# Two products from one moving operand: merge gates, branch and output projections, delta gates

## The chip, the cores and the metric

The kernel runs on one core of a Trainium2 chip. The metric is device time in microseconds (us) of one launch. Engines in the text: PE is TensorE (matmuls; PEld its weight loads), DVE is VectorE, ACT is ScalarE, POOL is GpSimd, SP issues the DMAs. Matmuls write PSUM, in banks of 512 f32 columns on 128 partitions; ACT and DVE read the banks and write SBUF.

## The reference

All data are f32, 256 tokens of width 1024. First a block of a hybrid mixer (two attention kinds, whose outputs of width 512 are raised to the model width, gated and summed) and product-key experts; then, with 16 meta tokens ahead, a banded attention layer and a gated delta-rule layer. The lines whose computation the change touches:

```
# hybrid mixer: y_fox, y_nsa are the outputs of the two attentions
g = sigmoid(merge_logit).reshape(B_, S_, 2, 1024)         # merge_logit: columns of h @ w_in
ys = stack([y_fox, y_nsa], axis=2)
up = einsum('bsnc,ncd->bsnd', ys, w_branch)
merged = sum(g * up, axis=2)
return merged @ w_out                                      # the caller adds the residual
# delta layer
u = rms_norm(h, norm_w) @ w_in                             # q, k, v, z, b, a
... gated delta rule of q, k, v gives o ...
... the normalised o is multiplied by silu(z), then o @ w_out
```

## The kernel before

**Products.** To keep f32 accuracy on PE, every f32 operand is split into a part `hi` (rounded to fp32r) and the rest `lo`, and a product is three: hi·hi, lo·hi, hi·lo (`mm3`, L277). The stationary operand is a weight block of 128x128, the moving one the activations transposed, [128 of the width, token columns]. `proj_t` (L284) makes one output block of 128x256 in PSUM: for each k (a 128-slice of the width) three matmuls of 256 columns.

**Weights.** `unit` (L263) brings one unit of weights, 128x1024 f32 (512 KB): a DMA by SP into `raw` (4 buffers), ACT copies it to `hi` (L269), DVE subtracts to get `lo` (L270); hi and lo have 3 buffers each. One unit is the weights of one output block over 8 k, or, in the branch projection, of two output blocks over 4 k.

**The stages in question.** They follow each other late in the mixer and in the second half of the delta layer. Merge gates (L670 to L676): 16 units, two of which fill the two halves of a bank (`pj_ps`, 2 buffers); DVE multiplies the bank by R (the token's norm) into `mg`, ACT takes tanh. Branch (L678 to L691): 8 units, for q = 0..3 one of each branch; a unit fills a bank with its two output blocks; DVE computes (mg + 1) * bank (scalar_tensor_tensor, L687) into `up`, sums the two branches' `up` (L690), and `split` (ACT L274, DVE L275) gives `me`, hi and lo. Output projection (L692 to L696): 8 units on `me`, two per bank; DVE computes 0.5 * bank + xT. Delta gates (`gates`, L1605): 16 units, each through `proj` into a bank of `pj`, and ACT takes silu (L1330) straight from it; between them stand the matmuls and copies of the delta rule's substitution (`r`, `pr`, `zt`, `rn`).

**Order.** The program is written in Python in this order, and the framework fixes each engine's order of instructions at build time by its own estimates of times (`schedule_with_timeline_sim=True`, L1782). A buffer is reused after its last reader (`reuse_waits="tile"`, L200), by a semaphore; each engine takes its instructions in the fixed order.

Of the kernel before, what the change touches and what calls it, by code (L numbers as in the profile page):

```python
# [6 lines left out]
F32 = mybir.dt.float32  # L7
F32R = mybir.dt.float32r
# [3 lines left out]
AF = mybir.ActivationFunctionType  # L12
ALU = mybir.AluOpType
# [4 lines left out]
T = 256  # L18
M = 16
L = M + T  # L20
KD = D // 128
# [169 lines left out]
class Net:  # L191
# [81 lines left out]
    def split(self, hi, lo, src):  # L273
        self.nc.scalar.activation(hi, src, AF.Copy)  # L274
        self.nc.vector.tensor_sub(lo, src, hi)  # L275

    def mm3(self, out, a, b, start, stop, **kw):  # L277

        mm = self.nc.tensor.matmul
        mm(out, a[0], b[0], start=start, stop=False, **kw)  # L280
        mm(out, a[0], b[1], start=False, stop=False, **kw)  # L281
        mm(out, a[1], b[0], start=False, stop=stop, **kw)  # L282
# [92 lines left out]
    def mixer(self, WARM=12):  # L375
        nc, ap = self.nc, self.ap
# [3 lines left out]
        h1T = self.hp.tile([128, KD, T], F32, name="h1T")  # L380
        self.h1T = h1T
        yf = self.xh.tile([128, 2, 4, T], F32R, name="yf", tag="xh")
        yn = self.xl.tile([128, 2, 4, T], F32R, name="yn", tag="xl")
        A = self.pool("mixA", side="right")
        W = self.pool("mixW", side="right")
        pj = self.pool("pj", bufs=2, space=PSUM)
# [3 lines left out]

        xT = A.tile([128, KD, T], F32, name="xT")
        nc.sync.dma_start(xT[:, 0:2], ap["xT"][:, 0:2])
        hh = A.tile([128, KD, T], F32R, name="hh", tag="ah")
        hl = A.tile([128, KD, T], F32R, name="hl", tag="al")
        units = iter(range(ap["w_t1"].shape[0]))
        nxt = lambda: self.unit(ap["w_t1"][next(units)])
        w = nxt()
# [3 lines left out]
        ps = sc.tile([128, 512], F32, name="warm", tag="sc")  # L401
# [5 lines left out]
        hT = (hh, hl)  # L407
# [7 lines left out]
        for m in range(0, 4, 2):  # L415
            ps = pj.tile([128, 2, T], F32, name="pj_ps", tag="pj")
            for j in range(2):
                self.proj_t(ps[:, j], nxt(), hT)
            if m == 0:
                R = A.tile([128, T], F32, name="R")  # L420
                self.rstd(R, xT, T, W, sc, "sc", load=False)
                Rb = R[:, None, :].to_broadcast([128, 2, T])
# [9 lines left out]
                z = W.tile([8, T], F32, name="fz")  # L432
# [26 lines left out]
            for f in range(2):  # L459
                s = slice(64 * f, 64 * f + 64)  # L460
                nc.vector.tensor_mul(kz[s, 2 * m + f:2 * m + 4:2], ps[s], Rb[s])
        for m in range(0, 4, 2):
            ps = pj.tile([128, 2, T], F32, name="pj_ps", tag="pj")
# [37 lines left out]
        yf = yf[:, 0], yf[:, 1]  # L501
        for i in range(2):
            n = 128 * (i + 1)
            ti = slice(i * 128, n)
            nh = 512 // n
            y = yp.tile([128, 4, 128], F32, name="y_ps", tag="yf")
            for h0 in range(0, 8, nh):
                ps = sc.tile([128, nh, n], F32, name="sc_ps", tag="sc")
                for j in range(nh):
                    h = h0 + j  # L510
# [9 lines left out]
                for j in range(nh):  # L520
                    h = h0 + j
# [147 lines left out]

        mg = A.tile([128, 16, T], F32, name="mg", tag="mg")  # L670
        for b in range(0, 16, 2):
            ps = pj.tile([128, 2, T], F32, name="pj_ps", tag="pj")
            for j in range(2):
                self.proj_t(ps[:, j], nxt(), hT)
            nc.vector.tensor_mul(mg[:, b:b + 2], ps, Rb)
            nc.scalar.activation(mg[:, b:b + 2], mg[:, b:b + 2], AF.Tanh, scale=0.5)  # L676

        me = [A.tile([128, KD, T], F32R, name="me" + n, tag="a" + n) for n in ("h", "l")]  # L678
        for q in range(4):
            ups = []  # L680
            for br, yy in ((0, yf), (1, yn)):
                w = self.unit(ap["w_br"][2 * q + br])
                ps = pj.tile([128, 2, T], F32, name="pj_ps", tag="pj")
                for j in range(2):
                    self.proj_t(ps[:, j], w, yy, ks=range(4), off=j * 512)
                up = W.tile([128, 2, T], F32, name="up", bufs=3)
                nc.vector.scalar_tensor_tensor(up, mg[:, 8 * br + 2 * q:8 * br + 2 * q + 2], 1.0, ps,  # L687
                                               op0=ALU.add, op1=ALU.mult)
                ups.append(up)
            nc.vector.tensor_add(ups[0], ups[0], ups[1])  # L690
            self.split(me[0][:, 2 * q:2 * q + 2], me[1][:, 2 * q:2 * q + 2], ups[0])  # L691
        for b in range(0, KD, 2):  # L692
            ps = pj.tile([128, 2, T], F32, name="pj_ps", tag="pj")
            for j in range(2):
                self.proj_t(ps[:, j], self.unit(ap["w_o1"][b + j]), me)
            nc.vector.scalar_tensor_tensor(h1T[:, b:b + 2], ps, 0.5, xT[:, b:b + 2], op0=ALU.mult, op1=ALU.add)  # L696
        self.dump("h1T", h1T)
        self.x2 = (self.xh.tile([128, KD, T], F32R, name="x2h", tag="xh"),
                   self.xl.tile([128, KD, T], F32R, name="x2l", tag="xl"))
# [527 lines left out]
    def delta(self, NZ=2, AH=4, KN=8, SS=1, SR=3, SW=3):  # L1227
# [17 lines left out]

        nh, nl = [A.tile([128, KD, L], F32R, name=n) for n in ("nh3", "nl3")]
        gd = self.d("g_dn")

        def normalise(k):
# [4 lines left out]
        def proj(ts=slice(0, L)):  # L1256
            ps = pj.tile([128, 512], F32, name="pj_ps", tag="pj")
            n = ts.stop - ts.start
            u = next(units)
            a = (hh, hl) if u <= KN else (nh, nl)  # L1260
            self.proj_t(ps[:, :n], self.unit(ap["w_t3"][u]), (a[0][:, :, ts], a[1][:, :, ts]))
            return ps[:, :n]
# [64 lines left out]
        def silu(raw, after=None, src=None):  # L1327

            with self.tc.issue_after(self.last), self.tc.issue_after(after or self.last):
                return nc.scalar.activation(raw, raw if src is None else src, AF.Silu).ins  # L1330
# [273 lines left out]

        def gates(z):  # L1605
            for j in range(4):
                silu(z[:, j], src=proj(slice(M, L)))
                yield

        sz = []  # L1610
# [175 lines left out]
```

## Time and profile before

| | us |
|---|---|
| median of 3 runs | 1470.3 (1469.41 to 1471.21) |
| the profiled execution | 1475.74 |
| its span | 1473.7 |
| PE busy in the span | 1445.8 (98%) |
| DVE busy | 1067.3 (72%) |
| ACT busy | 797.2 (54%) |

The times of single instructions come from the profiled execution. PE's busy time is modelled at the ends of matmuls, which overlap; the distance between starts is the pace. "a<-b" is the tile written and the tiles read; "128x256" is partitions by columns; a bracket at the end of a timeline row is the idle time of the engine before the instruction and who ended it.

### The profile page before, as it was taken

To read this page: it belongs to the slowest core of one execution; us is meant where nothing else is said; L and a number is where in the kernel's file an instruction comes from. 1 tells how busy PE (TensorE), PEld (TensorE's weight loads), DVE (VectorE), ACT (ScalarE), POOL (GpSimd) and SP (SyncE) were. 2 spreads that over 40 slices of the span, in tenths; PEclk is the share of its full clock that TensorE was granted. 3 is DMA by queue.
4 is the path that set the end of the run, shared out by engine and by line. 5 is a ranking of instruction groups with operands and counts; after the bars stand their busy time and mean duration, and the time that the engine had idled before them with its cause. 6 is when DMAs were issued, how large, how long until landed. Compare 5 with 4: busy or idle time off the path is not lost.

```text
span 1473.7 us, 27105 instructions
## 1 busy us (share of the span) xinstructions
PE 1445.8 (98%) x10635; PEld 1325.1 (90%) x10635; DVE 1067.3 (72%) x2124; ACT 797.2 (54%) x1372; POOL 73.5 (5%) x106
## 2 busy tenths in 40 slices
PE   9999999999999999999999999999999989999998
PEld 8788999999999999999888888888898989899777
DVE  7666577789948888998555555555876798985466
ACT  5566445545544444444444445454686667764364
POOL 0000000000000000000000000000113024000020
PEclk9999999999999999999999999999999999999899
DMA  6442464555655555555666666666442445435013
GB/s 229 141 146 85 143 186 150 173 167 171 195 178 159 162 154 171 157 151 170 195 190 197 193 192 197 198 189 197 143 126 76 145 129 158 144 127 156 21 43 114
DMA packets 72223, 229.19 MB, mean 156 GB/s; under 512 B 16048, under 2 KB 16464, under 8 KB 72096
## 3 DMA queue, kind: packets, MB, share of 16 engines
q1 hardware_dynamic: 71408, 225.69, 50.1%
q8 instruction: 83, 1.36, 0.4%
q0 software_dynamic: 400, 1.46, 0.3%
q10 hardware_dynamic: 288, 0.33, 0.1%
q14 instruction: 44, 0.36, 0.1%
HBM read 225.31 MB, written 2.13 MB: 154 GB/s over the span
## 4 chain that ended last, share of the span: by engine, by line
PE 93%; ACT 3%; DVE 2%; issue 1%; DMA 1%; POOL 0%; SPq 0%; ACTq 0%; DVEq 0%
PE pu_ps L280 10%; PE pu_ps L281 9%; PE pu_ps L282 9%; PE acc L280 8%; PE acc L281 8%; PE acc L282 8%; PE pj_ps L280 8%; PE pj_ps L282 8%; PE pj_ps L281 8%; PE pt_ps L898 2%; PE out L280 1%; PE tr_ps L366 1%; PE out L281 1%; PE out L282 1%; ACT hi L269 1%
## 5 line engine op out<-in xcount | busy, mean ns | idle before, releaser
L269 ACT ACTIVATE hi<-raw 128x1024 fp32r<-128x1024 f32 x422 | 445.8, 1058 | 432.2 <-PE pu_ps L281 167.8
L270 DVE TENSOR_TENSOR lo<-raw,hi 128x1024 fp32r<-128x1024 f32 x422 | 518.6, 1230 | 198.8 <-ACT hi L269 197.3
L280 PE MATMUL pu_ps<-x2h,hi 128*128 128x256 f32 x1152 | 330.8, 288 | 0.1
L281 PE MATMUL pu_ps<-x2l,hi 128*128 128x256 f32 x1152 | 326.4, 284 | 0.2 <-DVE x2l L275 0.2
L282 PE MATMUL pu_ps<-x2h,lo 128*128 128x256 f32 x1152 | 325.9, 283 | 0.0
L281 PEld LDWEIGHTS pu_ps<-x2l,hi 128*128 128x128 f32 x1152 | 221.0, 192 | 0.4 <-DVE x2l L275 0.4
L280 PEld LDWEIGHTS pu_ps<-x2h,hi 128*128 128x128 f32 x1152 | 220.5, 192 | 0.3 <-ACT x2h L274 0.3
L282 PEld LDWEIGHTS pu_ps<-x2h,lo 128*128 128x128 f32 x1152 | 220.7, 192 | 0.0
L281 PE MATMUL acc<-lo,ch 128*128 128x512 f32 x512 | 198.8, 389 | 0.0
L282 PE MATMUL acc<-hi,cl 128*128 128x512 f32 x512 | 198.2, 389 | 0.0
L280 PE MATMUL acc<-hi,ch 128*128 128x512 f32 x512 | 139.0, 389 | 0.0
L280 PE MATMUL pj_ps<-hh,hi 128*128 128x256 f32 (+1 forms) x432 | 125.7, 295 | 5.0 <-DVE cpad L1310 2.6
L282 PE MATMUL pj_ps<-hh,lo 128*128 128x256 f32 (+1 forms) x432 | 126.0, 293 | 0.5 <-DVE lo L270 0.5
L281 PE MATMUL pj_ps<-hl,hi 128*128 128x256 f32 (+1 forms) x432 | 125.9, 293 | 0.7 <-DVE hl L326 0.6
L282 PEld LDWEIGHTS acc<-hi,cl 128*128 128x128 f32 x512 | 96.1, 188 | 20.0
L281 PEld LDWEIGHTS acc<-lo,ch 128*128 128x128 f32 x512 | 96.1, 188 | 19.9
L280 PEld LDWEIGHTS acc<-hi,ch 128*128 128x128 f32 x512 | 96.0, 188 | 19.8
L280 PE MATMUL pj_ps<-nh,hi 128*128 128x256 f32 (+2 forms) x320 | 93.3, 292 | 1.6 <-ACT craw L1314 1.5
L281 PE MATMUL pj_ps<-nl,hi 128*128 128x256 f32 (+2 forms) x320 | 92.8, 290 | 0.0
L282 PE MATMUL pj_ps<-nh,lo 128*128 128x256 f32 (+2 forms) x320 | 92.1, 288 | 0.0
L280 PEld LDWEIGHTS pj_ps<-hh,hi 128*128 128x128 f32 x432 | 81.7, 191 | 7.2 <-issue 3.2
L281 PEld LDWEIGHTS pj_ps<-hl,hi 128*128 128x128 f32 x432 | 82.3, 191 | 2.0 <-DVE hl L326 1.1
(563 smaller groups left out, 2439.0 us busy)
## 6 DMA issues: line engine op xcount, KB each, us to landing
raw<-w_u SPq DMA_DIRECT2D x128, 512.0 KB, 3.7
raw<-w_v SPq DMA_DIRECT2D x128, 512.0 KB, 3.7
raw<-w_t SPq DMA_DIRECT2D x106, 512.0 KB, 3.7
raw<-w_o SPq DMA_DIRECT2D x32, 512.0 KB, 3.7
raw<-w_q SPq DMA_DIRECT2D x16, 512.0 KB, 3.7
raw<-w_br SPq DMA_DIRECT2D x8, 512.0 KB, 3.6
raw<-w_c SPq DMA_DIRECT2D x4, 512.0 KB, 3.8
xT<-xT SPq DMA_DIRECT2D x4, 256.0 KB, 5.2
```

The source lines that it names most:

```text
L269: nc.scalar.activation(hi, raw, AF.Copy)
L270: self.residual = (eng or nc.vector).tensor_sub(lo, raw, hi).ins
L280: mm(out, a[0], b[0], start=start, stop=False, **kw)
L281: mm(out, a[0], b[1], start=False, stop=False, **kw)
L282: mm(out, a[1], b[0], start=False, stop=stop, **kw)
L366: nc.tensor.transpose(tp[:, j], b, self.c("ident"))
L898: nc.tensor.matmul(ps[:, j], at[:, r, j // 2, :, j % 2], bt[:, j // 2, :, j % 2], start=j == 0 and r == 0, stop=r == 1, skip_group_check=True)
```

## The change

A new helper `proj_2` gives, for each k, one matmul of the weight's hi with the moving operand's hi and lo side by side (512 columns, into both halves of a bank), and one of the weight's lo with the moving hi (256 columns, into the first half). `whole_of` makes the output block of it: ACT copies the first half to SBUF, DVE adds the second. Merge gates, branch, output projection and delta gates use it; a bank then holds one output block instead of two. The tiles of the activations are laid out with hi and lo next to each other for each k.

```
@@ -274,6 +274,21 @@
         self.nc.scalar.activation(hi, src, AF.Copy)
         self.nc.vector.tensor_sub(lo, src, hi)
 
+    def proj_2(self, ps, w, act, ks=range(KD), off=0):
+
+
+        mm = self.nc.tensor.matmul
+        ks = list(ks)
+        for j, k in enumerate(ks):
+            s = slice(off + j * 128, off + (j + 1) * 128)
+            mm(ps, w[0][:, s], act(k), start=j == 0, stop=False, skip_group_check=True)
+            mm(ps[:, 0], w[1][:, s], act(k)[:, 0], start=False, stop=j == len(ks) - 1, skip_group_check=True)
+
+    def whole_of(self, dst, ps):
+
+        self.nc.scalar.activation(dst, ps[:, 0], AF.Copy)
+        self.nc.vector.tensor_add(dst, dst, ps[:, 1])
+
     def mm3(self, out, a, b, start, stop, **kw):
 
         mm = self.nc.tensor.matmul
@@ -381,6 +396,7 @@
         self.h1T = h1T
         yf = self.xh.tile([128, 2, 4, T], F32R, name="yf", tag="xh")
         yn = self.xl.tile([128, 2, 4, T], F32R, name="yn", tag="xl")
+        both = yf, yn
         A = self.pool("mixA", side="right")
         W = self.pool("mixW", side="right")
         pj = self.pool("pj", bufs=2, space=PSUM)
@@ -390,8 +406,8 @@
 
         xT = A.tile([128, KD, T], F32, name="xT")
         nc.sync.dma_start(xT[:, 0:2], ap["xT"][:, 0:2])
-        hh = A.tile([128, KD, T], F32R, name="hh", tag="ah")
-        hl = A.tile([128, KD, T], F32R, name="hl", tag="al")
+        hb = A.tile([128, KD, 2, T], F32R, name="hh", tag="a")
+        hh, hl = hb[:, :, 0], hb[:, :, 1]
         units = iter(range(ap["w_t1"].shape[0]))
         nxt = lambda: self.unit(ap["w_t1"][next(units)])
         w = nxt()
@@ -669,31 +685,34 @@
 
         mg = A.tile([128, 16, T], F32, name="mg", tag="mg")
         for b in range(0, 16, 2):
-            ps = pj.tile([128, 2, T], F32, name="pj_ps", tag="pj")
             for j in range(2):
-                self.proj_t(ps[:, j], nxt(), hT)
-            nc.vector.tensor_mul(mg[:, b:b + 2], ps, Rb)
+                ps = pj.tile([128, 2, T], F32, name="pj_ps", tag="pj")
+                self.proj_2(ps, nxt(), lambda k: hb[:, k])
+                self.whole_of(mg[:, b + j], ps)
+            nc.vector.tensor_mul(mg[:, b:b + 2], mg[:, b:b + 2], Rb)
             nc.scalar.activation(mg[:, b:b + 2], mg[:, b:b + 2], AF.Tanh, scale=0.5)
 
-        me = [A.tile([128, KD, T], F32R, name="me" + n, tag="a" + n) for n in ("h", "l")]
+        mb = A.tile([128, KD, 2, T], F32R, name="me", tag="a")
+        me = mb[:, :, 0], mb[:, :, 1]
         for q in range(4):
             ups = []
-            for br, yy in ((0, yf), (1, yn)):
+            for br, yy in enumerate(both):
                 w = self.unit(ap["w_br"][2 * q + br])
-                ps = pj.tile([128, 2, T], F32, name="pj_ps", tag="pj")
+                up = W.tile([128, 2, T], F32, name="up", bufs=3)
                 for j in range(2):
-                    self.proj_t(ps[:, j], w, yy, ks=range(4), off=j * 512)
-                up = W.tile([128, 2, T], F32, name="up", bufs=3)
-                nc.vector.scalar_tensor_tensor(up, mg[:, 8 * br + 2 * q:8 * br + 2 * q + 2], 1.0, ps,
+                    ps = pj.tile([128, 2, T], F32, name="pj_ps", tag="pj")
+                    self.proj_2(ps, w, lambda k: yy[:, :, k], ks=range(4), off=j * 512)
+                    self.whole_of(up[:, j], ps)
+                nc.vector.scalar_tensor_tensor(up, mg[:, 8 * br + 2 * q:8 * br + 2 * q + 2], 1.0, up,
                                                op0=ALU.add, op1=ALU.mult)
                 ups.append(up)
             nc.vector.tensor_add(ups[0], ups[0], ups[1])
             self.split(me[0][:, 2 * q:2 * q + 2], me[1][:, 2 * q:2 * q + 2], ups[0])
-        for b in range(0, KD, 2):
+        for b in range(KD):
             ps = pj.tile([128, 2, T], F32, name="pj_ps", tag="pj")
-            for j in range(2):
-                self.proj_t(ps[:, j], self.unit(ap["w_o1"][b + j]), me)
-            nc.vector.scalar_tensor_tensor(h1T[:, b:b + 2], ps, 0.5, xT[:, b:b + 2], op0=ALU.mult, op1=ALU.add)
+            self.proj_2(ps, self.unit(ap["w_o1"][b]), lambda k: mb[:, k])
+            for f, x in enumerate((xT, h1T)):
+                nc.vector.scalar_tensor_tensor(h1T[:, b], ps[:, f], 0.5, x[:, b], op0=ALU.mult, op1=ALU.add)
         self.dump("h1T", h1T)
         self.x2 = (self.xh.tile([128, KD, T], F32R, name="x2h", tag="xh"),
                    self.xl.tile([128, KD, T], F32R, name="x2l", tag="xl"))
@@ -1245,7 +1264,8 @@
 
 
 
-        nh, nl = [A.tile([128, KD, L], F32R, name=n) for n in ("nh3", "nl3")]
+        nb = A.tile([128, KD, 2, L], F32R, name="nh3")
+        nh, nl = nb[:, :, 0], nb[:, :, 1]
         gd = self.d("g_dn")
 
         def normalise(k):
@@ -1604,7 +1624,10 @@
 
         def gates(z):
             for j in range(4):
-                silu(z[:, j], src=proj(slice(M, L)))
+                ps = pj.tile([128, 2, T], F32, name="pj_ps", tag="pj")
+                self.proj_2(ps, self.unit(ap["w_t3"][next(units)]), lambda k: nb[:, k, :, M:])
+                self.whole_of(z[:, j], ps)
+                silu(z[:, j])
                 yield
 
         sz = []
```

Where instructions stand on the engines. DVE in the branch stage, before: `up_2137` is the first branch unit's result, its bank `pj_ps_2112`, and `lo_2211` is the lo part of the weights three units on.

```order
L687 SCALAR_TENSOR_TENSOR up_2137<-mg_1599,pj_ps_2112 128x512
L270 TENSOR_TENSOR lo_2211<-raw_2208,hi_2210 128x1024
L687 SCALAR_TENSOR_TENSOR up_2170<-mg_1599,pj_ps_2145 128x512
L690 TENSOR_TENSOR up_2137<-up_2137,up_2170 128x512
L270 TENSOR_TENSOR lo_2247<-raw_2244,hi_2246 128x1024
L275 TENSOR_TENSOR mel_2105<-up_2137,meh_2104 128x512
```

The same place on DVE after: `up_2022` is the first unit's result, `pj_ps_2023` and `pj_ps_2034` are the banks of its two halves, and `lo_2112` is the lo part of the weights three units on.

```order
L290 TENSOR_TENSOR up_2022<-up_2022,pj_ps_2023 128x256
L692 TENSOR_TENSOR mg_1598<-mg_1598,R_237 128x512
L270 TENSOR_TENSOR lo_2112<-raw_2109,hi_2111 128x1024
L290 TENSOR_TENSOR up_2022<-up_2022,pj_ps_2034 128x256
L290 TENSOR_TENSOR up_2052<-up_2052,pj_ps_2053 128x256
L706 SCALAR_TENSOR_TENSOR up_2022<-mg_1598,up_2022 128x512
L270 TENSOR_TENSOR lo_2145<-raw_2142,hi_2144 128x1024
L290 TENSOR_TENSOR up_2052<-up_2052,pj_ps_2064 128x256
L290 TENSOR_TENSOR up_2085<-up_2085,pj_ps_2086 128x256
L706 SCALAR_TENSOR_TENSOR up_2052<-mg_1598,up_2052 128x512
L709 TENSOR_TENSOR up_2022<-up_2022,up_2052 128x512
```

Before, the one read of the first unit's bank stands ahead of the lo three units on; after, of its two reads the second (`pj_ps_2034`) stands behind it, and the multiply by `mg` behind both; the next unit repeats it with `pj_ps_2064` behind `lo_2145`.

ACT at the same place, before: hi of the weights and, between, the tanh and the split of `me`.

```order
L269 ACTIVATE hi_2177<-raw_2175 128x1024
L676 ACTIVATE mg_1599<-mg_1599 128x512
L269 ACTIVATE hi_2210<-raw_2208 128x1024
L269 ACTIVATE hi_2246<-raw_2244 128x1024
L274 ACTIVATE meh_2104<-up_2137 128x512
L269 ACTIVATE hi_2279<-raw_2277 128x1024
```

ACT after, with the copies of the banks' first halves; `hi_2111` belongs to `lo_2112`.

```order
L289 ACTIVATE up_2022<-pj_ps_2023 128x256
L693 ACTIVATE mg_1598<-mg_1598 128x512
L269 ACTIVATE hi_2111<-raw_2109 128x1024
L289 ACTIVATE up_2022<-pj_ps_2034 128x256
L289 ACTIVATE up_2052<-pj_ps_2053 128x256
L269 ACTIVATE hi_2144<-raw_2142 128x1024
L289 ACTIVATE up_2052<-pj_ps_2064 128x256
L289 ACTIVATE up_2085<-pj_ps_2086 128x256
```

ACT did not read these banks before; after, the copy of the first unit's second half stands behind hi three units on.

ACT at the last delta gate, before: `z12` is the last group of gates, L1330 its silu, L226 the table load for what follows.

```order
L269 ACTIVATE hi_16292<-raw_16290 128x1024
L1533 ACTIVATE pr_14784<-zt_15419 32x4x32
L1330 ACTIVATE z12_15847<-pj_ps_15944 128x256
L1542 ACTIVATE rn_15473<-r2_15468 64x256
L1522 ACTIVATE pr_14784<-r1_15517 32x4x32 x2
L226 ACT_TABLE_LOAD
L1533 ACTIVATE pr_14784<-zt_15544 32x4x32
L1542 ACTIVATE rn_15566<-r2_15561 64x256
```

The same place after: L289 is the copy, L1350 the silu, now in SBUF.

```order
L289 ACTIVATE z12_15612<-pj_ps_15691 128x256
L1562 ACTIVATE rn_15268<-r2_15263 64x256
L1542 ACTIVATE pr_14621<-r1_15306 32x4x32 x2
L226 ACT_TABLE_LOAD
L1350 ACT_TABLE_LOAD
L1350 ACTIVATE z12_15612<-z12_15612 128x256
L1553 ACTIVATE pr_14621<-zt_15333 32x4x32
```

The silu came ahead of the table load before; after, it stands behind it and brings a load of its own.

## Rows read from the trace of the kernel before

**Rows 1.** The page: busy us, share and instructions; then the chain's shares.

```profile
PE 1445.8 (98%) x10635; PEld 1325.1 (90%) x10635; DVE 1067.3 (72%) x2124; ACT 797.2 (54%) x1372; POOL 73.5 (5%) x106
...
PE 93%; ACT 3%; DVE 2%; issue 1%; DMA 1%; POOL 0%; SPq 0%; ACTq 0%; DVEq 0%
```

**Rows 2.** Windows by stage: length, busy us (instructions), granted clock, DMA share, GB/s.

```profile
184.00:210.00 26.00, 26.00 (x217) 25.83 (x215) 21.12 (x26) 12.61 (x14) 0.53 (x1) 1.00 0.62 184
1303.00:1340.00 37.00, 37.00 (x326) 34.24 (x326) 26.86 (x56) 20.22 (x37) 0.00 (x0) 1.00 0.55 157
```

**Rows 3.** Longest waits of PE, 112 to 240 us, then 1265 to 1345 us.

```profile
PE acc L725 <- ACT rms_r L234: 0.6, 1, 0.6
...
PE tp L1582 <- ACT v L1573: 1.4, 1, 1.4
```

**Rows 4.** Timeline, merge gates to first branch units: start, us, engine, instruction.

```profile
184.04 0.28 PE L281 MATMUL pj_ps<-hl,hi 128*128 128x256 f32 x1
...
184.16 0.28 PE L282 MATMUL pj_ps<-hh,lo 128*128 128x256 f32 x1
...
184.28 0.28 PE L280 MATMUL pj_ps<-yf,hi 128*128 128x256 f32 x1
...
184.41 1.06 ACT L269 ACTIVATE hi<-raw 128x1024 fp32r<-128x1024 f32 x1 [1.79 <-PE pj_ps L281]
184.48 0.69 DVE L675 TENSOR_TENSOR mg<-pj_ps,R 128x512 f32<-128x512 f32 x1 [0.60 <-PE pj_ps L282]
...
185.50 1.23 DVE L270 TENSOR_TENSOR lo<-raw,hi 128x1024 fp32r<-128x1024 f32 x1 [0.33 <-ACT hi L269]
...
187.15 0.28 PE L280 MATMUL pj_ps<-yn,hi 128*128 128x256 f32 x1
```

**Rows 5.** Timeline of PE: matmuls of 512 columns in two places.

```profile
98.00 0.39 PE L281 MATMUL pj_ps<-lo,hh 128*128 128x512 f32 x1
...
102.18 0.39 PE L281 MATMUL pj_ps<-lo,hh 128*128 128x512 f32 x1
...
900.60 0.39 PE L281 MATMUL acc<-lo,ch 128*128 128x512 f32 x1
...
902.18 0.39 PE L282 MATMUL acc<-hi,cl 128*128 128x512 f32 x1
```

**Rows 6.** Groups by line and form, 112 to 240 us: busy, mean ns, idle before.

```profile
L675 DVE TENSOR_TENSOR mg<-pj_ps,R 128x512 f32<-128x512 f32 x8 | 5.5, 690 | 5.8 <-PE pj_ps L282 5.8
L687 DVE SCALAR_TENSOR_TENSOR up<-mg,pj_ps 128x512 f32<-128x512 f32 x8 | 5.5, 686 | 3.1 <-PE pj_ps L282 3.1
...
L275 DVE TENSOR_TENSOR mel<-up,meh 128x512 fp32r<-128x512 f32 x4 | 2.7, 686 | 0.0
...
L274 ACT ACTIVATE meh<-up 128x512 fp32r<-128x512 f32 x4 | 2.5, 633 | 1.8 <-DVE up L690 1.8
```

**Rows 7.** Single lines: duration min/median/max ns, first and last start, forms.

```profile
L771 ACT ACTIVATE q<-pu_ps x16: 367/367/373, 242.6 to 319.4; 128x256 f32<-128x256 f32 x16
...
L559 DVE TENSOR_TENSOR cz<-pj_ps,R x2: 416/420/425, 78.5 to 84.0; 128x256 f32<-128x256 f32 x2
...
L1325 DVE SCALAR_TENSOR_TENSOR qT<-cpad,dat_sb,qT x24: 464/474/521, 1205.1 to 1238.1; 128x256 f32<-128x256 f32 x24
...
L1330 ACT ACTIVATE z<-pj_ps x16: 357/368/386, 1303.6 to 1363.9; 128x256 f32<-128x256 f32 x16
```

**Rows 8.** Timeline of ACT: a table load among the delta gates.

```profile
1365.67 1.28 ACT L226 ACT_TABLE_LOAD   x1
```

**Rows 9.** Windows of 2 us on the delta gates' last units; PEclk is the clock.

```profile
1362.00:1364.00 2.00, 1.40 (x31) 1.03 (x30) 0.90 (x3) 1.44 (x3) 0.00 (x0) 1.00 0.62 244
1364.00:1366.00 2.00, 1.85 (x33) 1.60 (x34) 1.87 (x5) 1.52 (x5) 0.20 (x1) 0.96 0.12 16
1366.00:1368.00 2.00, 2.00 (x14) 1.17 (x16) 0.48 (x2) 0.96 (x1) 0.00 (x0) 0.50 0.73 246
```

## The prediction

> **What bounds the kernel now.** I read the page first. TensorE (PE) is busy 98% of the span and carries 93% of the chain that ended last; VectorE (DVE) is busy 1067.3 us of 1473.7, ScalarE (ACT) less [rows 1]. So the kernel is as long as its matmul stream, as long as nothing holds that stream up. The windows by stage say where it is held up: in the branch stage (184 to 210 us) PE is busy 26.00 of 26.00 us, and DVE 21.12; at 1303 to 1340 us, the first half of the delta gates, PE 37.00 and DVE 26.86 [rows 2]. The waits of PE say the same with names: from 112 to 240 us its longest wait is 0.6 us, from 1265 to 1345 us 1.4 us, and neither is for a PSUM bank of the projections [rows 3]. The reader should take from this that time leaves the kernel only if the PE stream gets shorter, and comes in wherever PE has to wait for a bank. The change does something on both sides.
>
> **Shorter matmul stream.** Merge gates 16 units of 8 k, branch 8 units of 2 x 4 k, output projection 8 units, delta gates 16: 48 units, 384 k. Each k was three matmuls of 256 columns and becomes one of 512 and one of 256. The first branch unit starts at 184.28 and the next at 187.15 [rows 4]: 24 matmuls in 2.87 us, 0.1196 us each, 0.359 per k. A 512-column matmul on two parts is in the trace: 18 starts from 98.00 to 102.18, 0.232 us each; 7 from 900.60 to 902.18, 0.226 us [rows 5]. So a k becomes 0.226 + 0.120 = 0.345, or 0.232 + 0.120 = 0.352; I take the middle, 0.348. The gain is 0.007 to 0.013 us per k, 2.7 to 5.2 us over 384 if nothing else happens; with 0.348, a unit takes 2.79 us in place of 2.87 and half a branch unit 1.39.
>
> The Trainium skill ("TensorE: Matmul & The Clock Gate", section "Wait — 56ns, not 53.3ns?") gives a full-clock matmul its columns over 2.4 GHz plus about 2.5 ns. By it a merged pair saves one fixed cost, 2.5 ns, and the stream 1 us in all. The rows disagree: 120 ns against its 109 for 256 columns, 226 to 232 against its 216 for 512. By the page the sum below would be some 3 us higher.
>
> **What empties a bank.** Before, one DVE instruction read the bank: multiply or scalar_tensor_tensor of 128x512, 690 and 686 ns [rows 6], 0.32 us after the last matmul's start (184.16 to 184.48 [rows 4]), and a bank held two outputs, so it was wanted back only after the other bank's two units of work. Now a bank holds one output of one unit (of half a branch unit), and it is emptied by an ACT copy of half 0 and a DVE add of half 1. Prices of such forms: ACT from PSUM 128x256 367 ns, DVE tensor_tensor with a PSUM operand 420 ns, scalar_tensor_tensor of 128x256 474 ns [rows 7]. That work itself is small. What decides is what it is queued behind.
>
> The weight tiles hi and lo have three buffers, so hi of unit X+3 may be written only when unit X's matmuls with hi are over: at 184.41 hi starts, released by the matmul that started at 184.04, 0.37 us later, and lo follows 0.03 us behind hi's end [rows 4]. In the changed order ACT has hi of X+3 ahead of the copy of X's second half, and DVE has lo of X+3 ahead of the add of it (the order pieces of ACT and DVE in the section on the change). Both engines take their instructions in order. So the second half's bank is given back only after a whole hi and lo.
>
> *Branch, 8 units.* From the start of a unit's second half: the last w_hi matmul starts at 3 x 0.348 = 1.04; released 0.48 later (0.37 for a matmul of 0.28 us, and a 512-column one takes 0.39 [rows 4, 5]): 1.52. hi 1.06 to 2.58, 0.03, lo 1.23 to 3.84, add 0.42 to 4.26; with about 0.07 to hand over, less the bit by which instructions on an engine overlap, PE may have the bank at about 4.25. It wants this bank for the second half of the next unit: half a unit after the end of this half, at 2.79. It waits 1.46. So the period is 4.25 in place of 2.87: +1.38 x 8 = +11.0 us. This is no waiting that a reserve absorbs: the next hi waits in its turn for the unit that waited, so every one of the eight pays. (DVE's work per unit, lo 1.23, two adds 0.84, the 0.69 stt, half a sum and half a split 0.69, is 3.4 of 4.25 and fits.)
>
> *Into the output projection.* Its k = 6, 7 wait for the last sum and split. That chain, behind the last add (2.86 after the last half's end), is stt 0.69, sum about 0.69 (an operation of the same size), split on ACT 0.63 and on DVE 0.69 [rows 6]: about 5.6 us after that end. The 12 matmuls on k 0 to 5 of unit 0 cover 2.09 us, those of unit 1 (which needs the late bank, at 2.86) 2.09 more from there, to 4.95. Holes of 0.77 and 0.65: +1.4 us, where before PE had none [rows 3].
>
> *Merge gates, 16 units of 8 k.* Same queueing (copy behind hi of X+3, add behind lo), but two whole units pass before a bank is wanted. Last w_hi at 7 x 0.348 = 2.44, released 2.92, hi to 3.98, lo from 4.01 to 5.24, add to 5.66; wanted at 2 x 2.79 = 5.57. About 0.1 late in two units: 2.83 in place of 2.87, −0.6 us for 16 units.
>
> *Output projection.* Here the two stt stand ahead of the next lo on DVE; they take 0.95 us within a unit's 2.79, so no wait: 8 x −0.08 = −0.6.
>
> *Delta gates, 16 units.* Matmul gain 16 x −0.08 = −1.3. Their 16 silu start from 1303.6 to 1363.9 [rows 7], one in 4.0 us, since other matmuls of the delta rule lie between the units; two units take 8.0 us, more than the 5.66 of the chain above: banks come back in time. The silu, formerly ACT alone out of the bank, is now copy, add, silu: 16 x 0.42 = 6.7 us more on DVE, 16 x 0.37 = 5.9 more on ACT (a silu of this size took 368 ns [rows 7]), and the silu stands on ACT ahead of the delta substitution's copies, which wait there for its add. The last silu now comes behind the table load for the later stages, so ACT loads once more (the last order pieces there): 1.28 us [rows 8], where PE works from hand to mouth. Bounds: −1.3 (all hidden) to +5 (the load, and 0.25 us of delay at each gate unit: 1.28 + 16 x 0.25 less the gain); nearer to hidden, since ACT is busy 20.22 of 37 us there [rows 2]: I take +0.5.
>
> **Sum.** −0.6 + 11.0 + 1.4 − 0.6 + 0.5 = +11.7 us. The profiled execution took 1475.74 us (span 1473.7), which becomes 1487.4; the median of the runs is 5.4 below that execution, so 1470.3 + 11.7 = 1482.0.
>
> **Rivals.**
> (a) *The banks come back in time and the shorter stream shows*: 384 x −0.010 = −3.9, 1466.4; with the bounds 1465.1 to 1467.6. For it: PE fills its span, and the copy and add are 0.8 us of work in 2.8. Against: the order of the queues. It would need hi of X+3 not to wait for unit X, and the row at 184.41 shows that wait.
> (b) *The two cancel*: within 0.2% of the time before, which is about what a measurement of this kernel can tell from no change (1467.4 to 1473.2). It needs the branch's wait to be a third of what I work out, or a cost of the merged matmul that is much below the rows.
> (c) *The clock falls.* With waits of 1.46 in 4.25 us, PE is busy 66% of the branch stage. In the trace a stretch in which PE was busy 1.40 of 2 us was followed by a granted clock of 0.96 and then 0.50, that is 1.2 GHz in place of 2.4 [rows 9]. If that happens in the branch stage, a half unit takes 2.78, the chain is 2.09 + 0.9 + 1.06 + 0.03 + 1.23 + 0.42 = 5.7 a unit: 1.45 x 8 = 11.6 more, 1493.6; half of that if it falls in the middle. Against: after the 1.40 came only a few us of low clock, and the waits here are short. The Trainium skill names such a case (same page, "A second HAM failure mode: psum-queue depth-cycling"): a matmul stream that cycles through PSUM banks and pauses between groups has its clock gate swing between the levels. No row here shows it for pauses of this length.
> (d) *The delta gates cost more*: substitution copies late behind each silu, +5 instead of +0.5: 1486.5.
>
> **How the numbers follow.** The forecast as told, 1478 to 1486, 0.70; (a) 0.05; (b) 0.03; (c) 0.12; (d) 0.10. The likeliest gives 1482.0. The range leaves out (a), (b) and the far end of (c): 1475 to 1491. Faster by over 0.2% is (a), 0.05; within 0.2% (b), 0.03; slower 0.92.
>
> **What would show it.** After: PE's waits should have a group "projection matmul, branch, waits for DVE" (the add), 8 of about 1.46 us, 12 us in all, each with lo of the unit three ahead ending just before the add; PE's busy share in the branch stage should fall from 1.00 to about two thirds, and the stage should last some 34 us in place of 23. A wait of under 0.2 us per pair of merge gates; two holes of 0.6 to 0.8 us at the head of the output projection; none later in it. Inside the merge gates 512-column starts 0.226 to 0.232 apart. Wrong would be: branch units still 2.8 us apart (then hi does not wait as I say), or a granted clock under 1.00 between 184 and 225 us.

## The result, and the profile after

| | before | after |
|---|---|---|
| median of runs, us | 1470.76 (1469.41 to 1473.72) | 1489.47 (1488.54 to 1490.35) |
| ratio, 95% interval | | 1.0125 [1.0109, 1.0142] |
| profiled execution, span, us | 1473.7 | 1488.2 |

Slower by 18.7 us; 11.7 had been forecast. The time lies inside the stated range (1475 to 1491), but above the 1478 to 1486 that had been given 0.70. The spans differ by 14.5 only, because the profiled execution before had more low clock than most: every execution comes with the mean granted clock of TensorE, and that one had 0.992. Of 94 executions of the kernel before that ran beside the experiments (a 95th, of 2479.7 us at 0.696, is left out), 59 had a mean clock of 0.997 or more and a median of 1469.9, 35 a lower clock and 1474.1. The changed kernel had 0.994 or 0.995 in all of its four. The twelve executions of before at 0.994 or 0.995 have a median of 1475.0: at equal clock the change costs 14.4 us, and about 4 of the 18.7 are that the low clock came in every execution.

First the place where the forecast put the loss. The waits of PE, changed kernel, 100 to 260 us (engine, line, released by: us in total, times, longest):

```profile
PE pj_ps L284 <- DVE up L290: 9.2, 8, 1.3
PE pj_ps L284 <- DVE mg L290: 1.1, 1, 1.1
...
PE pj_ps L284 <- DVE me L275: 0.5, 1, 0.5
PE pj_ps L284 <- DVE h1T L715: 0.4, 1, 0.4
```

Before, no projection waited here [rows 3]. One of these waits in the timeline of the changed kernel:

```profile
187.17 0.40 PE L284 MATMUL pj_ps<-yn,hi 128*128 128x512 f32 x1
187.30 1.06 ACT L269 ACTIVATE hi<-raw 128x1024 fp32r<-128x1024 f32 x1
...
188.26 0.90 ACT L289 ACTIVATE up<-pj_ps 128x256 f32<-128x256 f32 x2
188.39 1.23 DVE L270 TENSOR_TENSOR lo<-raw,hi 128x1024 fp32r<-128x1024 f32 x1 [1.86 <-ACT hi L269]
188.47 0.28 PE L285 MATMUL pj_ps<-yn,lo 128*128 128x256 f32 x1
189.53 0.74 DVE L290 TENSOR_TENSOR up<-up,pj_ps 128x256 f32<-128x256 f32 x2
...
190.00 0.50 PE L284 MATMUL pj_ps<-yn,hi 128*128 128x512 f32 x1 [1.26 <-DVE up L290]
...
191.16 0.40 PE L284 MATMUL pj_ps<-yn,hi 128*128 128x512 f32 x1
...
191.65 1.06 ACT L269 ACTIVATE hi<-raw 128x1024 fp32r<-128x1024 f32 x1 [2.48 <-PE pj_ps L284]
```

Read the wait at 190.00 upwards: PE stood from 188.75 until the first of the two adds was over, for the bank of a half whose matmuls had ended at about 187.3; that add stood behind lo, and lo needs hi. The last two rows show the same place one unit on, with the wait of hi: it stood 2.48 us for the unit's own matmuls and started 0.49 us after the last of them with w_hi (191.16), as the hi at 187.30 did (behind 186.81). The next waits of PE for the add end at 194.35 and 198.70, so the period is 4.35 us.

The stages are measured by the first matmul of the start-up's norm, of the branch, of the output projection, and of the norm behind it. Before (start us, us, engine, instruction):

```profile
13.97 0.48 PE L307 MATMUL rms_ps<-rms_sq,ones 128*128 128x256 f32 x1
...
207.31 0.28 PE L280 MATMUL pj_ps<-meh,hi 128*128 128x256 f32 x1
...
230.51 0.38 PE L307 MATMUL rms_ps<-rms_acc,ones 128*128 128x256 f32 x1
```

After:

```profile
13.15 0.81 PE L322 MATMUL rms_ps<-rms_sq,ones 128*128 128x256 f32 x3
...
182.83 0.50 PE L284 MATMUL pj_ps<-yf,hi 128*128 128x512 f32 x1
...
217.44 0.39 PE L284 MATMUL pj_ps<-me,hi 128*128 128x512 f32 x1
...
242.03 0.38 PE L322 MATMUL rms_ps<-rms_acc,ones 128*128 128x256 f32 x1
```

With the branch's start of before, 184.28 [rows 4]: up to the branch −0.6 (−1.45, of which −0.82 lies ahead of 14 us, where before had more low clock), branch 34.61 in place of 23.03, +11.6, output projection 24.59 in place of 23.20, +1.4. So 12.3 us by the end of the mixer; the rest of the 18.7 comes later. These two profiles show only 3.0 of it there (from the norm behind the mixer to the end, 1243.2 us before and 1246.2 after), and both have low clock in it.

There, at the last delta gate, ACT of the changed kernel:

```profile
1380.13 1.28 ACT L226 ACT_TABLE_LOAD   x1
1381.42 1.28 ACT L1350 ACT_TABLE_LOAD   x1
1382.71 0.42 ACT L1350 ACTIVATE z<-z 128x256 f32<-128x256 f32 x1
1383.15 0.27 ACT L1553 ACTIVATE pr<-zt 32x128 f32<-32x128 f32 x1
```

the wait of PE behind it (1.63 us, until 1383.47):

```profile
PE r L1559 <- ACT pr L1553: 1.6, 1, 1.6
```

and the windows around it (length, busy us of PE, PEld, DVE, ACT, POOL; then the granted clock):

```profile
1382.00:1384.00 2.00, 0.53 (x8) 0.53 (x8) 0.95 (x4) 1.38 (x3) 0.00 (x0) 1.00 0.59 231
1384.00:1386.00 2.00, 2.00 (x11) 1.24 (x10) 0.96 (x4) 0.38 (x1) 0.20 (x1) 0.67 0.00 0
1386.00:1388.00 2.00, 2.00 (x13) 1.88 (x12) 1.10 (x4) 0.00 (x0) 0.00 (x0) 0.50 0.04 8
```

The copy of the substitution (`pr`) stands behind both loads; PE waits 1.63 us for it, is busy 0.53 of 2 us, and is then granted half its clock. The profiled execution before, with one load and a wait of 0.6 us for the copy, was granted half its clock at this place too [rows 9]; so the fall alone does not show what the second load did.

### The profile page after: what moved, and what is told of

Read it like the earlier page. It is cut to its first block, busy times and chain, and to the rows that moved or that the text cites. A ratio compares the mean times of both kernels' runs of the same rounds, so it can differ in the third digit from the quotient of the medians.

```text
span 1488.2 us, 26433 instructions
## 1 busy us (share of the span) xinstructions
PE 1445.9 (97%) x10251; PEld 1305.3 (88%) x10251; DVE 1085.9 (73%) x2184; ACT 813.8 (55%) x1421; POOL 72.3 (5%) x106
## 3 DMA queue, kind: packets, MB, share of 16 engines
q0 software_dynamic: 400, 1.46, 0.3%
## 4 chain that ended last, share of the span: by engine, by line
PE 90%; ACT 4%; DVE 3%; issue 2%; DMA 1%; POOL 0%; SPq 0%; ACTq 0%; DVEq 0%
PE pu_ps L295 9%; PE pu_ps L296 9%; PE pu_ps L297 9%; PE acc L295 8%; PE acc L296 8%; PE acc L297 8%; PE pj_ps L284 5%; PE pj_ps L296 4%; PE pj_ps L295 4%; PE pj_ps L297 4%; PE pj_ps L285 3%; PE pt_ps L917 2%; ACT hi L269 2%; DVE lo L270 1%; PE out L295 1%
## 5 line engine op out<-in xcount | busy, mean ns | idle before, releaser
L295 PE MATMUL pj_ps<-hh,hi 128*128 128x272 f32 (+1 forms) x304 | 89.1, 299 | 4.2 <-DVE cpad L1330 2.6
L297 PE MATMUL pj_ps<-hh,lo 128*128 128x272 f32 (+1 forms) x304 | 89.3, 296 | 0.8 <-DVE lo L270 0.8
L296 PE MATMUL pj_ps<-hl,hi 128*128 128x272 f32 x216 | 64.7, 301 | 0.7 <-DVE hl L341 0.6
L295 PEld LDWEIGHTS pj_ps<-hh,hi 128*128 128x128 f32 x304 | 58.0, 193 | 5.5 <-issue 2.8
L297 PEld LDWEIGHTS pj_ps<-hh,lo 128*128 128x128 f32 x304 | 58.4, 193 | 1.9 <-DVE lo L270 1.0
L295 PE MATMUL pj_ps<-nh,hi 128*128 128x272 f32 (+1 forms) x192 | 56.0, 292 | 1.5 <-ACT craw L1334 1.4
L296 PE MATMUL pj_ps<-nh,hi 128*128 128x272 f32 (+1 forms) x192 | 56.4, 294 | 0.0
L297 PE MATMUL pj_ps<-nh,lo 128*128 128x272 f32 (+1 forms) x192 | 55.8, 291 | 0.0
```

## The experiments

All times are medians in us against the kernel before on the same chip; the clock is the mean granted clock over a kernel's executions, lowest to highest.

| run | us | ratio, 95% interval | clock |
|---|---|---|---|
| e1 mixer parts only | 1483.43 | 1.0082 [1.0059, 1.0105] | 0.996 to 0.999 |
| e2 delta gates only | 1478.11 | 1.0046 [1.0032, 1.0060] | 0.992 to 0.994 |
| e3 four banks | 1473.85 | 1.0026 [1.0013, 1.0038] | 0.994 to 0.999 |
| e4 no branch | 1469.25 | 0.9985 [0.9972, 0.9999] | 0.994 to 0.999 |
| e5 one load | 1472.47 | 1.0016 [1.0007, 1.0024] | 0.996 to 0.999 |
| e6 late silu | 1475.71 | 1.0035 [1.0021, 1.0049] | 0.991 to 0.997 |
| e7 three matmuls | 1474.73 | 1.0025 [1.0013, 1.0037] | 0.991 to 0.998 |
| e8 best | 1469.17 | 0.9996 [0.9985, 1.0006] | 0.995 to 0.999 |
| e9 emptied first | 1473.53 | 1.0023 [1.0009, 1.0037] | 0.992 to 0.998 |
| e10 all mended | 1477.92 | 1.0038 [1.0022, 1.0054] | 0.992 to 0.999 |
| e11 change, one load | 1486.51 | 1.0110 [1.0084, 1.0136] | 0.994 to 0.997 |
| e12 before, two loads | 1476.81 | 1.0034 [1.0023, 1.0045] | 0.992 to 0.997 |

**The parts alone.** e1 undoes the hunk in `gates`, e2 the hunks in the mixer, e4 the branch's hunk and that in `gates`.

> Merge gates, branch and output projection as changed, delta gates as before. Theory (the second half's bank is given back only behind hi and lo of the unit three ahead): 8 waits of 1.25 us in the branch stage, which lasts 34.6 us in place of 23.0, and two holes after it; +12 us in all, about 1483. Rival (the loss is mostly in the delta gates or in the clock, and the waits in the branch stage are partly given back later): under +8 us, below 1479.

> Only the delta gates as changed. Theory after the result (18.7 us slower in all, some 12 of it up to the experts): the gates cost +4 to +7 us, 1475 to 1478, by the silu that waits on ACT for its add, by the second table load, and by low clock behind it. Rival (the forecast's +0.5: the rest of the loss is a few us of low clock here and there that have nothing to do with the gates): 1470 to 1472.

> Merge gates and output projection as changed, branch and delta gates as before. Theory: a whole unit's bank has time to come back; merge gates -0.65 us (as the trace after shows), output projection -0.6: 1469 to 1470. Rival (copies and adds on ACT and DVE cost what the matmuls gain, wherever they stand): 1471 to 1473.

e1 is 13.3 above before, close to the 12.3 of the stages. e2 is 8.0 above, just past the upper end of its theory (1478), and its clock is low in all of 7 executions. The parts add up to 21.3, the whole is 18.7: the losses do not simply add. e4 is a little faster, as expected; the whole loss in the mixer is the branch, with the holes that it leaves behind it.

**What holds the bank.** e3 gives the second halves other banks; e9 keeps the banks and changes the order of issue:

```
e3: -  ps = pj.tile([128, 2, T], F32, name="pj_ps", tag="pj")
    +  ps = (sc if j else pj).tile([128, 2, T], F32, name="pj_ps", tag="sc" if j else "pj")
e9: +  with self.tc.issue_after(emptied[n][0]), self.tc.issue_after(emptied[n][1]):
    +      return self.unit(src)    # emptied[n]: copy and add of the unit three back
```

> As e1, but in the branch stage the second halves go to two other banks (the pool of the attention scores), so that a bank is wanted back a whole unit later. Theory: the chain takes 4.25 us from the start of the second half and the bank is now wanted after 5.6, so the 8 waits are gone, the branch stage takes 8 x 2.79 = 22.3 us, and only the holes at the head of the output projection (up to 1.4 us) stand against a gain of 384 - 128 = 256 k at 0.010 us: 1468.5 to 1470.5. Rival (the branch loses by copy, add and in-place multiply on engines, or by the matmul form, whatever the banks): still +8 to +12 us.

> As e1 (merge gates, branch and output projection as changed, delta gates as before, two banks), but hi and lo of the unit three ahead are issued behind the copy and the add of the second half. Theory (only their place in the queues holds the bank): the bank is free 0.3 + 0.37 + 0.42 = 1.1 us after the half's end and wanted after 1.39, so the 8 waits of 1.25 us go without another bank; DVE's work per branch unit, about 3.0 us with the overlap of its instructions, is then what is left over a unit's 2.79: 1470 to 1472 against e1's 1483.4. Rival (two banks are too few for copy and add on two engines in any order): 1478 to 1484.

Either mend takes about 10 of e1's 13.3 us. Waits of PE, 184 to 240 us, e3 (the waits for the norm behind are left out):

```profile
PE pj_ps L284 <- DVE me L275: 1.9, 2, 1.5
PE pj_ps L284 <- DVE up L290: 1.7, 2, 1.2
...
PE pj_ps L284 <- DVE h1T L715: 0.4, 1, 0.4
```

and e9:

```profile
PE pj_ps L284 <- DVE up L290: 2.8, 7, 0.9
...
PE pj_ps L284 <- DVE h1T L726: 0.4, 1, 0.4
```

So the place in the queue held the bank: with the same two banks and the same work, only the order on ACT and DVE differs between e1 and e9; PE has its matmuls in the same order in both traces. (e3 is less clean: with other banks the framework also moved the branch's first half ahead of merge gates, to 179.95.) Both miss their forecasts, e3 by 3.4 us and e9 by 1.5. In e9's branch stage, one window:

```profile
184.00:211.00 27.00, 24.21 (x130) 19.45 (x129) 24.27 (x39) 16.28 (x30) 0.00 (x0) 1.00 0.52 158
```

DVE is busy 24.27 of 27 us: with the two adds it has some 3 us of work to a unit, and PE wants a unit every 2.8. So DVE is probably what is left, in e3 in a few long waits; no run tests that.

**The delta gates.** e5 leaves one call out (the table is loaded again behind the substitution anyway); e6 adds an order, e7 takes the matmuls apart again:

```
e5: -            self.logexp()              # at the end of values()
e6: as e5, and
    -                silu(z[:, j])
    +                if j:
    +                    silu(z[:, j - 1], after=copy)       # copy: that of unit j
e7: as e2, and
    -            mm(ps, w[0][:, s], act(k), start=j == 0, ...)
    +            for f in range(2):
    +                mm(ps[:, f], w[0][:, s], act(k)[:, f], start=j == 0, ...)
```

(In e7 a gate's sum lacks a part of its first k, since the second half is started before the first is complete; only its time is read.)

> As e2 (delta gates as changed, 1478.1), without the early table load behind the gates, which made ACT load the silu's table once more: two loads fewer, all else in the same order. Theory A (the two loads, 2.6 us on ACT while the substitution's copies wait, are the larger part, and they bring on the low clock): 1472 to 1474, mean clock 0.996 and above in most executions. Theory B (the silu's waits for its add, spread over the gates, are the larger part): 1476.5 to 1478, mean clock still 0.992 to 0.995.

> As e5, and each silu but the last of its four stands on ACT behind the next unit's copy, where its add is over, so that ACT does not wait for it. Theory B: the 11 waits of ACT for the add, 12.6 us in e2, shrink to those of the last of each four, and the time falls by 2 to 4 us against e5. Theory A: within 1 us of e5.

> Delta gates with copy, add and silu in SBUF, but with three matmuls of 256 columns into the two halves, and with one load only, as the order comes out. If the merged matmul takes away work that covered the substitution: 1 to 3 us faster than e5, with high clock. If the emptying alone costs: as e5, or the 1.3 us slower that the three matmuls take.

e5 is 5.6 us faster than e2 with two loads fewer and the same order, at 0.996 to 0.999 in place of 0.992 to 0.994: the time and the clock of theory A (the two ran on different chips; against before on its own chip, 8.0 became 2.3). The route that theory A gives is not in e2's trace:

```profile
1368.67 1.28 ACT L226 ACT_TABLE_LOAD   x1
1369.96 1.28 ACT L1348 ACT_TABLE_LOAD   x1
1371.25 0.42 ACT L1348 ACTIVATE z<-z 128x256 f32<-128x256 f32 x1
1371.69 0.27 ACT L1551 ACTIVATE pr<-zt 32x128 f32<-32x128 f32 x1
```

The wait of PE for that copy:

```profile
PE r L1557 <- ACT pr L1551: 0.5, 1, 0.5
```

and the windows ahead of it:

```profile
1366.00:1368.00 2.00, 1.21 (x26) 0.87 (x24) 1.04 (x4) 1.79 (x4) 0.20 (x1) 1.00 0.83 248
1368.00:1370.00 2.00, 1.88 (x11) 1.57 (x12) 1.75 (x3) 1.93 (x5) 0.00 (x0) 0.72 0.04 14
```

A mean of 0.72 over the second window is half clock from about 1368.9 on, which is 0.2 us after the first load's start and ahead of PE's wait behind the loads, which ends at 1372.01 and is 0.54 us long. PE had paused 0.91 us just before; in e5 it paused as long at the same work, and its clock stayed at 1.00. So leaving the loads out goes with the gain, and what brought the clock down in e2 is not shown.

Theory B falls: in e6 ACT waits 2.9 us for the adds in place of e2's 12.6, and the time is no better. Its median is 3.2 above e5, which theory A's "within 1 us" misses too, because half of its executions had 0.991 to 0.994; at 0.996 or 0.997 they took 1473.7 to 1475.1, and those of e5 at 0.996 1473.4 to 1474.9. Why its clock fell stays open, but e6 has no table load at the gates: the clock falls without one as well. e7 tells little: its executions spread from 1469.96 at 0.998 to 1477.38 at 0.992.

**Is it the loads?** e11 is the whole change with e5's edit. e12 is the kernel before with nothing but the order of the load and the last silu changed:

```
e12: -                silu(z[:, j], src=proj(slice(M, L)))
     +                src = proj(slice(M, L))
     +                if last: ... self.logexp()             # behind the silu before
     +                silu(z[:, j], after=self.table if last else None, src=src)
```

> The whole change, only without the early table load. If the load's 5.6 us (e2 to e5) are a loss of their own: 1483.5 to 1484.5, and a clock of 0.996 or more. If they came by chance of where the gates stood in e2: 1487 to 1490.

> The kernel before, with the early table load moved ahead of the last gate's silu, so that ACT loads the silu's table once more at that place, as in the changed kernel; no matmul, bank or add is changed. If two loads in a row where PE has little work are what costs the delta gates their 3 to 5.6 us, by the wait and by the low clock behind it: 1472 to 1476, mean clock under 0.997 in most executions. If the loads only hurt together with the copy, add and silu of the change: 1469.5 to 1471.5 and the clock as before.

e11 lies between its two forecasts: the mend gives the whole change 3.0 us, less than in e2. e12, just above its forecast, is 6.3 us slower than before without a single changed product, and 11 of its 12 executions had under 0.997 (10 of them 0.994 or less), where 7 of 17 of before on the same chip had (2 of them 0.994 or less). The two loads do not follow each other directly in e12; the second, with a silu, stands ahead of the copy:

```profile
1359.81 1.28 ACT L226 ACT_TABLE_LOAD   x1
...
1363.45 1.28 ACT L1330 ACT_TABLE_LOAD   x1
1364.75 0.38 ACT L1330 ACTIVATE z<-pj_ps 128x256 f32<-128x256 f32 x1
1365.15 0.27 ACT L1533 ACTIVATE pr<-zt 32x128 f32<-32x128 f32 x1
```

Its windows there:

```profile
1362.00:1366.00 4.00, 1.51 (x34) 1.27 (x34) 1.79 (x3) 2.99 (x4) 0.00 (x0) 0.95 0.30 108
1366.00:1379.00 13.00, 12.39 (x104) 9.70 (x103) 5.75 (x19) 2.70 (x8) 0.39 (x2) 0.50 0.13 42
```

and those of before, in its profiled execution:

```profile
1362.00:1366.00 4.00, 3.25 (x63) 2.63 (x62) 2.77 (x7) 2.95 (x7) 0.20 (x1) 0.98 0.37 130
1366.00:1379.00 13.00, 12.39 (x86) 9.95 (x85) 4.91 (x16) 2.74 (x6) 0.20 (x1) 0.50 0.12 39
```

In e12 PE was busy 1.51 of 4 us around the second load and then had half its clock for 13 us (1.2 GHz for 2.4). It waits once for 2.5 us for the copy (0.6 before). But the profiled execution before had the same 13 us at half clock, with one load. So the place of the loads adds a wait, and by the mean clocks it makes a fall that comes in some executions of before come in nearly all. What each is worth can be read from the profiles: us from the first to the last matmul of the delta layer's input projections (`pj_ps<-nh`; the gates are the last of them), from there to the end of the span, and the half clock in either (a fall in the idle time at the very end is left out).

| | projections | behind | half clock in them, us |
|---|---|---|---|
| before | 165.07 | 110.74 | 13.7 behind |
| e1 (gates as before) | 165.36 | 105.55 | none |
| e12 | 164.45 | 112.85 | 13.7 behind |
| e2 | 168.24 | 110.70 | 3.4 and 13.7 |
| e5 | 166.67 | 105.54 | none |
| e11 | 166.80 | 105.55 | none |
| after | 166.94 | 110.80 | 6.8 and 3.4, behind |

With the gates as before, the fall costs 5.2 us where it comes (110.74 less 105.55). In e12 the place of the loads adds 2.1 to that; the rest of its 6.3 fits a fall that comes more often. In e2 nothing is added to it. Copy, add and silu cost 1.3 to 1.6 us in the projections (e5, e11 and after against e1).

**Mended versions.**

> Merge gates and output projection as changed, branch and delta gates as before, and the early table load left out (the table is loaded once more behind the substitution anyway). e4 gave 0.85 us; the load is 1.28 us on ACT where PE has little work, so up to 1.3 more if it is on the path, nothing if not: 1467.5 to 1469.5 against 1470.1, and fewer executions with low clock.

> The whole change with both mends: the order of e9 and the one load of e5. If the two losses are separate: e9 plus 2.3 us, 1472 to 1474.5. If they share a cause (the clock, the transfers): 1476 and more.

e8 is e4 without the early load; it meets its forecast, and does not differ from e4 by what can be measured. e10 is e9 and e5 together: 7.2 us over before where 2.8 and 2.3 had been measured apart, which is its rival's range. In its profile the part behind the projections lasts 108.25 us, in e5's 105.54 and in e9's 105.58: 1.1 us come in the substitution, whose steps stand in another order there, and 1.6 from 3.4 us at half clock at 1423.5. No version beats the kernel before by more than e4's 0.15% [0.01%, 0.28%].

## Why the prediction was right, and where it was not

*Stream.* Five k in the changed merge gates, starts of the 512-column matmuls:

```profile
169.23 0.40 PE L284 MATMUL pj_ps<-hh,hi 128*128 128x512 f32 x1
...
170.99 0.39 PE L284 MATMUL pj_ps<-hh,hi 128*128 128x512 f32 x1
```

0.352 us per k, the upper of the two bounds (taken: 0.348), so the gain is 0.007 per k, not 0.010. The stretch up to the branch, with the merge gates, came out at −0.6, as forecast; e4 shows 0.85 us for merge gates and output projection, where 1.2 was forecast.

*Branch.* Right in mechanism and nearly in size: +11.6 for +11.0. The waits are 1.15 to 1.27 rather than 1.46, the first matmul after each takes 0.50 us where others take 0.40, and the period is 4.35 for 4.25. e9 shows that it is the order and not the banks.

*Output projection.* Three holes, 0.53, 0.49 and 0.36, for the two of 0.77 and 0.65; the stage +1.4 for +0.8.

*Delta gates.* Here a term was mis-sized: "I take +0.5", with +5 as its bound (whose own terms, 1.28 + 16 x 0.25 less 1.3, make +4.0). It measured 5.4 us in the whole change (18.7 less e1's 13.3) and 8.0 alone (e2). By the table above, the whole change loses 1.6 us against e1 up to the last gate and 5.2 behind it. Two steps failed.

The first is that the matmuls' gain of 1.3 stays and copy, add and silu are nearly hidden. The waits of PE, changed kernel, 1313 to 1400 us:

```profile
PE mv L1607 <- ACT va L1599: 1.0, 1, 1.0
PE tp L1602 <- ACT v L1593: 0.9, 1, 0.9
PE z L1565 <- ACT rn L1562: 0.9, 1, 0.9
PE pj_ps L284 <- DVE z L290: 0.4, 1, 0.4
```

The waits for va, v and z are not in e1's profile, and make 2.3 us before the last gate; the one for rn (0.2 in e1) follows a silu that had waited 1.78 us for its add, the mechanism that the prediction named.

The second is the price of the second table load: 1.28 us, its own duration. In the whole change the place of the loads is worth 3.0 us by the medians (e11) and 5.2 in the profile, with the wait of 1.63 us and 10.2 us at half clock; in the kernel before it is worth 6.3 (e12), in e2 5.6. That it goes into a wait and into half clock can be read from the profiles; why the clock falls in one execution and not in another is not shown.

*Rival (c), the clock.* It fell, but not where I looked, and "only a few us of low clock" misread [rows 9], whose fall went on for 13.7 us. In the branch stage PE was busy 24.17 of 34 us with eight pauses of about 1.2 us, and the granted clock was 1.00 throughout:

```profile
184.00:218.00 34.00, 24.17 (x127) 19.10 (x126) 23.78 (x38) 15.00 (x29) 0.00 (x0) 1.00 0.41 133
```

The case of the Trainium skill, a clock that swings where a stream cycles through PSUM banks ("TensorE: Matmul & The Clock Gate", "A second HAM failure mode: psum-queue depth-cycling"), did not show here. It fell where [rows 9] had shown it, in the thin work of the substitution, which the change made thinner, and in two more places, for 3.4 us each (from 1197 and 1436). Rivals (a) and (b) fell with the branch; for (b), a third of the branch's wait would not have been little enough: 0.7 + 3.7 = 4.4 us is over 0.2%.

*The sum* was 7.0 us short of the 18.7: 1.1 of it in the mixer's stages (12.3 for 11.2), the rest behind them, where the delta gates are, with the clock different from run to run. Rival (d), at 0.10, had the place right and was still 3.0 us short (1486.5). That the time lies inside the range is in part luck: the room above (d) had been left for (c) in the branch stage, where the clock did not fall.

## What to carry to other kernels

Before a PSUM bank is emptied by two instructions instead of one, look at what each is queued behind on its engine: here the 0.8 us of copy and add cost 1.45 us of PE per unit because a weight split that waited for the same unit stood ahead, and issuing the emptying first gave 10 us back. A table load is not priced by its 1.28 us alone: where PE has thin work, see whether an activation has slipped behind a preload (worth 3 us in the whole change, 6 in the kernel before), and what the granted clock does afterwards, over several executions. Compare executions at the same mean granted clock before differences of a few us are put down to an edit, and look in the trace whether the clock fell before or after what is blamed for it.

## What the runs showed of the hardware

- Executions of one kernel differ by their granted clock: before, 1469.9 at 0.997 and above against 1474.1 below (94 executions); stretches at half clock lasted 3.4 to 13.7 us each.
- Half clock came behind PE busy 1.51 of 4 us (e12) and 0.53 of 2 us (after), not in the branch stage, with pauses of 1.2 us in 4.35 and PE at 71%. The same work with the same pause of 0.91 us was followed by half clock in e2's profile and by full clock in e5's.
- The same instructions with one table load had 13.7 us of half clock at one place in the profiled execution before, and none there in e1's.
- In the branch stage, the first matmul of 512 columns after a wait took 0.50 us in place of 0.40.
- Two table loads in a row took 1.28 us each, back to back (1380.13 and 1381.42, after).
